# Stationary weights of the first MLP projection: every other column, a distance of its own for each unit

## The chip, the cores and the metric

The kernel runs on one core of a Trainium2 chip. The metric is the device time of one execution in microseconds; it is the median of several runs. TensorE (PE) multiplies: a weight load (PEld) puts a block of 128 x 128 into the array, the *stationary* operand, and a matmul then streams up to 512 columns of the *moving* operand past it, with sums in PSUM. VectorE (DVE) and ScalarE (ACT) prepare operands and take results out, GpSimd (POOL) does little here, and SyncE (SP) issues the transfers from HBM to SBUF.

## The reference

One decoder layer for 256 positions of width 2048, in fp32. A combined projection feeds three branches (gated DeltaNet, HGRN2, attention into 256 memory tokens), which are gated, added and projected; then follows the MLP, which the change is about:

```python
        h2 = rmsnorm(x, g_pre_mlp[l])
        m = jnp.square(jax.nn.relu(h2 @ w_mlp_in[l])) @ w_mlp_out[l]
        x = x + rmsnorm(m, g_post_mlp[l])
```

`w_mlp_in` is 2048 x 8192, `w_mlp_out` 8192 x 2048.

## The kernel before

**Two halves of each number.** Each fp32 operand is split into a high part (rounded to the fast matmul format, `fp32r`) and a low part, the rest. A product is high x high + high x low + low x high. ACT makes the high part (a cast), DVE the low part (a subtraction); for weights these are `wh`, `wl`, or in the MLP `oh`, `ol`, for the normed activations `h2h` holds both parts side by side.

**The first projection.** It has 16 *units* of 512 columns of `w_mlp_in`; two units make an *e* of 1024 columns, and there are eight of these. In unit 0 the activations are stationary. In units 1 to 15 (`unit_stacked`) the weights are stationary. The 16 blocks of 128 rows (index `kt`) come two to a *group* (`KG = 2`), so a unit has 8 groups, loaded by a DMA of 512 KB each into one of six `raw` buffers. `products_joined` works on two groups at a time. For each of the four column blocks `c` and each `kt` there is a *wide* product, the high block against 512 columns (the high and the low activations), and a *narrow* one, the low block against the 256 columns of the high activations. Wide ones of both groups come in a row of 32, then narrow ones in a row of 32, and the next pair of groups in turned order, so that wide follows wide. A unit has 64 wide and 64 narrow products; 15 units have 960 of each. Block `c` of a group is `wh[:, j, c * P:(c + 1) * P]`, 128 adjacent columns.

**Where operands lie.** In the built program every moving buffer, `h2h`, starts at a place in the partition that leaves the remainder 128 modulo 256 bytes, and so does each high tile. The low tile has some columns to spare, and `shifted` lets it start `o` elements later: 16 elements (64 bytes) in this projection (`aside`), 0 in the second one. `pair_at` makes the six pairs of tiles that all MLP weights go through in turn, `operand` hands out the next.

**What becomes of the result.** PSUM bank `c` holds block `c` of the unit, with hidden columns as partitions and positions as columns. ACT and DVE add its halves, apply the squared ReLU, and split it into `mh` and `ml`. These are the stationary operands of the second projection, whose moving operands are rows of `w_mlp_out`: partition i of block `c` must meet the row that belongs to the same hidden column. `raw` loads two blocks of 128 rows side by side, `(k p) n -> p k n`: partition p holds row p of each block. Part of the second projection goes through seven products of sums of quadrants instead of eight (`seven`), which also go through `raw`. Unit 0 has its result with positions as partitions, and `gen_turn` transposes it on PE.

**Order.** The engines each run their own stream of instructions, recorded in program order with background work (`bg`, `tick`) let in between groups; transfers of the MLP weights are all on SP's queue. The second projection of one e stands behind the first projection of the next.

Of the kernel before, what the change touches and what calls it, by code (L numbers as in the profile page):

```python
# [11 lines left out]
F32R = mybir.dt.float32r  # L12
# [5 lines left out]
P = 128  # L18
D = 2048
S = 256  # L20
# [13 lines left out]
KG = 2  # L34
# [6 lines left out]
def tile_trunk(ctx: ExitStack, tc, a):  # L41
    nc = tc.nc
# [21 lines left out]
    V, A, T = Placed(nc.vector), Placed(nc.scalar), Placed(nc.tensor)  # L64
# [25 lines left out]
    def nm(s):  # L90
        cnt[0] += 1
        return f"{s}_{cnt[0]}"

    def g4(name, shape=(P, 1024), dt=F32):
        return gp.tile(list(shape), dt, tag="g", name=nm(name))
# [14 lines left out]
    def const(name, shape, dt=F32):  # L110
        return cst.tile(list(shape), dt, tag=name, name=name)
# [6 lines left out]
    ident = const("ident", [P, P])  # L118
# [69 lines left out]
    def tick(share=1.0):  # L188
        credit[0] += rate[0] * share
        n = int(credit[0])  # L190
        credit[0] -= n
        pump(n)
# [12 lines left out]
    def shifted(t, o):  # L205
        return t[:, o:o + KG * 512].rearrange("p (k n) -> p k n", k=KG)
# [3 lines left out]
    def low(aside):  # L210
        t = wp.tile([P, KG * 512 + 32], F32R, tag="wl", name=nm("wl"))
        odd = low_turn[0] % 2
        low_turn[0] += 1
        return shifted(t, 16 if aside else 32 * odd)

    def split_w(w, n, width=512, step=None, q=lambda i: i, home=None, aside=False):
        if home:
            wh, wl = home(aside)
        else:
            wh = wp.tile([P, KG, 512], F32R, tag="wh", name=nm("wh"))  # L220
            wl = low(aside)
        for j in range(0, n, step or n):
            js = slice(j, min(j + (step or n), n))
            q(A.copy(wh[:, js, 0:width], w[:, js, 0:width]))
            q(V.tensor_tensor(out=wl[:, js, 0:width], in0=w[:, js, 0:width],
                              in1=wh.bitcast(F32)[:, js, 0:width], op=ALU.subtract))
        return wh, wl

    def load_w(src, k0, n, c0, width=512, home=None, aside=False):
        return split_w(load_w_raw(src, k0, n, c0, width), n, width, home=home, aside=aside)  # L230

    def unit(act, nk, src, c0, r0=0, order=None, split=False, post=None, ws=None, load=None):

        if split:
            ps = [bank("mm") for _ in range(2)]
        else:
            both = pmm.tile([P, 1024], F32, tag="mm", name=nm("mm"))  # L240
            ps = [both[:, 0:512], both[:, 512:1024]]
        if order is None:
            order = [(g, None) for g in range(nk // KG)]
        ws = ws or {}
        for i, (g, tt) in enumerate(order):
            k0 = g * KG
            if g not in ws:
                ws[g] = load(src, r0 + k0, c0) if load else load_w(src, r0 + k0, KG, c0)
            wh, wl = ws[g]
            for j in range(KG):  # L250
                kt = k0 + j
                ah, al = act(kt)
                for t in range(NT) if tt is None else (tt,):
                    o = ps[t]
                    st, sl = ah[:, t * P:(t + 1) * P], al[:, t * P:(t + 1) * P]
                    T.matmul(o, st, wh[:, j, :], start=kt == 0, stop=False)
                    T.matmul(o, st, wl[:, j, :], start=False, stop=False)
                    T.matmul(o, sl, wh[:, j, :], start=False, stop=kt == nk - 1)
            tick()
            if post is not None and i + 1 in post:  # L260
                post[i + 1](ps)
        return ps if split else both

    def products_joined(ps, groups, nk, cs, turned):

        for wide in (0, 1) if turned else (1, 0):
            for k0, (wh, wl), both in groups:  # L270
                for c in cs:
                    for j in range(KG):
                        end = k0 + j == nk - 1 and wide == turned
                        if wide:
                            T.matmul(ps[c], wh[:, j, c * P:(c + 1) * P], both[j], start=k0 + j == 0, stop=end)
                        else:
                            T.matmul(ps[c][:, 0:S], wl[:, j, c * P:(c + 1) * P], both[j][:, 0:S], start=False, stop=end)
                yield

    def flat(b):  # L280
        return b.rearrange("p s n -> p (s n)")

    def unit_stacked(pairs, nk, src, c0, ps, load, ws):

        for gg in range(0, nk // KG, 2):
            groups = []
            for g in (gg, gg + 1):
                k0 = g * KG
                groups.append((k0, ws[g] if g in ws else load(src, k0, c0, True),
                               [flat(pairs[kt // 4][:, kt % 4]) for kt in range(k0, k0 + KG)]))  # L290
            for i, _ in enumerate(products_joined(ps, groups, nk, range(4), gg // 2 % 2)):
                tick(0.5)


# [35 lines left out]
    def split_psum(ps, hi, lo):  # L330
        A.copy(hi, ps)
        V.tensor_tensor(out=lo, in0=ps, in1=hi.bitcast(F32), op=ALU.subtract)
# [297 lines left out]
    for u in range(2):  # L630
        ps = unit(mem_act, KT, w_kv, 1024 + 512 * u) if u else first_unit(w_kv, 1024)
# [7 lines left out]
    for u in range(2):  # L639
        k = unit_joined(lambda kt: memB[kt // 2][:, kt % 2], w_kv, 512 * u)  # L640
# [664 lines left out]
    for hg in range(2):  # L1305
        k, g = forget(unit_joined(hboth, w_in, OFF_BF + 512 * hg), hg)
        q = unit_joined(hboth, w_in, OFF_BQ + 512 * hg)
        own_table(A.activation(q, q, AF.Silu))
        ps = unit(hact, KT, w_in, OFF_BI + 512 * hg)
# [73 lines left out]
    ahead = {}  # L1383

    def first_weights(ps):
        for g in range(2):
            ahead[g] = load_w(a["w_mlp_in"][0], g * KG, KG, 0,
                              home=lambda aside: tuple(g4(n, (P, KG, 512), F32R) for n in ("wh", "wl")))

    for c in range(4):  # L1390
        ys.append(g4("y1", (P, NT, 512)))
        if c < 3:
            ps = unit(mact, KT, a["w_out"][0], 512 * c)
# [6 lines left out]
        else:  # L1400
# [3 lines left out]
            ps = unit(mact, KT, a["w_out"][0], 512 * c, order=last, split=True,  # L1404
                      post={8: first_weights, 11: lambda ps: mix_last(ps, 0)})
# [23 lines left out]
    def at(pool, tag, dt):  # L1429
        return pool.tile([P, KG, 512], dt, tag=tag, name=tag, bufs=1)  # L1430

    def pair_at(pool, i):
        return at(pool, f"oh{i}", F32R), pool.tile([P, KG * 512 + 64], F32R, tag=f"ol{i}", name=f"ol{i}", bufs=1)

    pairs = [pair_at(wx, i) for i in range(2)]
    raws = [at(wx, "raw0", F32)]

    def wide_ring():
        for g in range(2):
            w = load_w_raw(a["w_mlp_in"][0], g * KG, KG, 512)  # L1440
            ahead[8 + g] = split_w(w, KG, home=operand, aside=True)
        weights.close()
        wy = ctx.enter_context(tc.tile_pool(name="wy", bufs=1, side="right", reuse_waits="tile"))
        raws.extend(at(wy, f"raw{i}", F32) for i in range(1, 5))
        raws.append(g4("raw5", (P, KG, 512)))
        pairs.extend(pair_at(wy, i) for i in range(2, 6))

    def operand(aside):
        pairs.append(pairs.pop(0))
        return pairs[-1][0], shifted(pairs[-1][1], 16 if aside else 0)  # L1450

    def raw(src, k0, c0):
        w = raws.pop(0)
        raws.append(w)
        nc.sync.dma_start(w, src[k0 * P:(k0 + KG) * P, c0:c0 + 512].rearrange("(k p) n -> p k n", p=P))
        return w

    def load_in(src, k0, c0, aside=False):
        return split_w(raw(src, k0, c0), KG, home=operand, aside=aside)

    h2act = act_of(h2T)
    stf = const("stf", [P, 8])
    out_r = a["out"][0].rearrange("(t p) n -> p t n", p=P)
    NE = DFF // 1024
    first = [(g, t) for t in range(NT) for g in range(4)] + [(g, None) for g in range(4, 8)]
    w_mo = a["w_mlp_out"][0]

    def gen_turn(r, rT, hi, lo):

        yield  # L1470
        pt = pmm.tile([P, 1024], F32, tag="mm", name=nm("mT"))
        for hh in range(2):
            for q in range(2):
                for t in range(NT):
                    k = t * 4 + hh * 2 + q
                    T.transpose(pt[:, hh * 512 + q * S + t * P:hh * 512 + q * S + (t + 1) * P],
                                r[:, k * P:(k + 1) * P], ident)
            p3 = pt[:, hh * 512:(hh + 1) * 512].rearrange("p (q s) -> p q s", q=2)
            split_psum(p3, hi[:, hh * 2:hh * 2 + 2, :], lo[:, hh * 2:hh * 2 + 2, :])
            A.copy(rT[:, hh * 2:hh * 2 + 2, :], p3)  # L1480
            yield
# [221 lines left out]
```

## Time and profile before

| | us |
|---|---|
| median of 3 runs (1776.69 to 1779.16) | 1776.71 |
| profiled execution, device time | 1777.77 |
| its span, first to last instruction | 1776.0 |
| PE busy | 1761.3 |
| weight loads busy (they overlap PE) | 1495.8 |
| DVE busy | 1303.4 |
| ACT busy | 961.8 |
| first projection, units 1 to 15: from start 1098.7 to 1682.8, between output products | 960 wide, 960 narrow |

A group's row in the profile names what was written, then what was read, the moving operand ahead of the stationary one: `mm<-h2h,oh` is a wide product, `mm<-h2h,ol` a narrow one. Behind the shape (rows * columns of the array, then the output) stand the count, the time in which at least one of the group was running, the mean length of one in ns, and the idle time ahead of them with what ended it. Lengths of matmuls overlap, since the next starts while one drains; the pitch from start to start is what counts, and it is read from the timeline.

### The profile page before, as it was taken

What the parts mean: (1) busy time and instruction counts of PE and PEld (TensorE: products, weight loads), DVE (VectorE), ACT (ScalarE), POOL (GpSimd) and SP (SyncE); (2) the same over time, 40 slices, a digit from 0 to 9 for tenths busy, and PEclk for the clock granted to TensorE, in tenths of its full rate; (3) what the DMA queues carried; (4) which work ended last, traced back from release to release, by engine and by line L of the source; (5) the groups of instructions that cost most, each with busy time, mean ns of one, the idle gap of its engine ahead of it and who ended that gap; (6) DMA issues with size and microseconds to landing.
All of it is one profiled execution on the core that took longest, in us unless ns stands there. A gap on an engine that the chain in (4) does not pass through costs nothing.

```text
span 1776.0 us, 23962 instructions
## 1 busy us (share of the span) xinstructions
PE 1761.3 (99%) x9053; PEld 1495.8 (84%) x9053; DVE 1303.4 (73%) x1764; ACT 961.8 (54%) x1217; POOL 58.0 (3%) x100
## 2 busy tenths in 40 slices
PE   9999999999999999999999999999999999999998
PEld 7888888888888888888888888888888888888886
DVE  6765768685859487698555557796979797969796
ACT  6644666454555475565444445665545464646453
POOL 1000000400030000000000000000000000000000
PEclk9999999999999999999999999999999999999999
DMA  8665555875587465555666665767767676767683
GB/s 265 214 193 166 168 160 165 220 216 159 161 216 210 135 190 166 158 174 168 188 189 189 235 222 198 233 228 237 229 226 249 220 250 214 257 204 250 212 295 144
DMA packets 188804, 362.84 MB, mean 204 GB/s; under 512 B 14456, under 2 KB 16272, under 8 KB 188304
## 3 DMA queue, kind: packets, MB, share of 16 engines
q1 hardware_dynamic: 181856, 351.32, 62.2%
q0 software_dynamic: 2304, 5.44, 1.5%
q10 hardware_dynamic: 4528, 4.54, 0.9%
q8 instruction: 71, 1.16, 0.3%
q14 instruction: 45, 0.37, 0.1%
HBM read 356.86 MB, written 4.39 MB: 203 GB/s over the span
## 4 chain that ended last, share of the span: by engine, by line
PE 77%; DVE 5%; issue 2%; DMA 1%; ACT 1%; DVEq 0%; POOLq 0%; POOL 0%; ACTq 0%
PE mm L56 73%; DVE ol L56 3%; PE pa L56 1%; DMA raw<-in_w_mlp_out 1%; DVE relu L56 1%; DVE raw L56 1%; PE kk L56 0%; DVE ml L56 0%; PE bo L56 0%; PE o L56 0%; PE pzt L56 0%; PE pw L56 0%; PE tr L56 0%; PE y L56 0%; PE oT L56 0%
## 5 line engine op out<-in xcount | busy, mean ns | idle before, releaser
L56 DVE TENSOR_TENSOR wl<-w,wh 128x1024 fp32r<-128x1024 f32 (+1 forms) x362 | 436.7, 1217 | 234.9 <-ACT wh L56 212.7
L56 ACT CAST wh<-w 128x1024 fp32r<-128x1024 f32 (+1 forms) x362 | 375.5, 1047 | 354.6 <-PE mm L56 293.2
L56 ACT CAST oh<-raw 128x1024 fp32r<-128x1024 f32 x288 | 299.3, 1053 | 274.8 <-PE mm L56 195.8
L56 DVE TENSOR_TENSOR ol<-raw,oh 128x1024 fp32r<-128x1024 f32 x288 | 343.2, 1221 | 95.5 <-ACT oh L56 65.3
L56 PE MATMUL mm<-wh,hh 128*128 128x512 f32 x1152 | 366.2, 392 | 0.0
L56 PEld LDWEIGHTS mm<-wh,hh 128*128 128x128 f32 x1152 | 216.1, 188 | 44.6 <-ACT wh L56 0.3
L56 PE MATMUL mm<-wl,hh 128*128 128x512 f32 x576 | 224.5, 390 | 0.0
L56 PE MATMUL mm<-h2h,oh 128*128 128x512 f32 x960 | 224.3, 390 | 0.0
L56 PEld LDWEIGHTS mm<-h2h,oh 128*128 128x128 f32 x960 | 178.1, 188 | 35.8
L56 PE MATMUL mm<-hh,wh 128*128 128x512 f32 x768 | 184.6, 391 | 0.8 <-ACT z L56 0.8
L56 PEld LDWEIGHTS mm<-hh,wh 128*128 128x128 f32 x768 | 140.6, 188 | 28.3 <-ACT z L56 1.0
L56 PE MATMUL mm<-ol,mh 128*128 128x512 f32 x372 | 145.3, 391 | 1.6 <-DVE ol L56 1.6
L56 PE MATMUL mm<-oh,mh 128*128 128x512 f32 x372 | 145.4, 391 | 0.0
L56 PE MATMUL mm<-oh,ml 128*128 128x512 f32 x372 | 143.8, 389 | 0.0
L56 PEld LDWEIGHTS mm<-wl,hh 128*128 128x128 f32 x576 | 108.2, 188 | 21.2
L56 PEld LDWEIGHTS mm<-h2h,ol 128*128 128x128 f32 x960 | 117.4, 189 | 3.0 <-DVE ol L56 0.7
L56 PE MATMUL mm<-h2h,ol 128*128 128x256 f32 x960 | 118.5, 281 | 0.5 <-DVE ol L56 0.5
L56 PEld LDWEIGHTS mm<-hh,wl 128*128 128x128 f32 x768 | 97.1, 188 | 3.4
L56 PE MATMUL mm<-hh,wl 128*128 128x256 f32 x768 | 99.7, 280 | 0.0
L56 PEld LDWEIGHTS mm<-ol,mh 128*128 128x128 f32 x372 | 69.8, 188 | 17.8 <-DVE ol L56 3.7
L56 PEld LDWEIGHTS mm<-oh,mh 128*128 128x128 f32 x372 | 69.8, 188 | 16.1 <-DVE acc L56 1.6
L56 PEld LDWEIGHTS mm<-oh,ml 128*128 128x128 f32 x372 | 69.8, 188 | 14.4
(363 smaller groups left out, 2208.7 us busy)
## 6 DMA issues: line engine op xcount, KB each, us to landing
w<-in_w_in SPq DMA_DIRECT2D x240, 512.0 KB, 4.2
raw<-in_w_mlp_out SPq DMA_DIRECT2D x170, 512.0 KB, 4.6
raw<-in_w_mlp_in SPq DMA_DIRECT2D x118, 512.0 KB, 4.8
w<-in_w_out SPq DMA_DIRECT2D x32, 512.0 KB, 4.2
w<-in_w_kv_mem SPq DMA_DIRECT2D x30, 512.0 KB, 5.0
w<-in_w_br_c SPq DMA_DIRECT2D x16, 512.0 KB, 3.6
w<-in_w_br_a SPq DMA_DIRECT2D x16, 512.0 KB, 4.3
w<-in_w_br_b SPq DMA_DIRECT2D x16, 512.0 KB, 3.6
```

What stands on the lines that cost most here:

```text
L56: ins = op(*args, **kwargs)
```

## The change

The stationary block `c` of a unit's group takes every other column of a half of 256: column 256 (c // 2) + 2 i + (c mod 2) for i = 0 to 127, a step of 8 bytes in SBUF. Both tiles of a pair now have 64 spare elements, and `places` gives each unit two starts, in elements, for its high and its low tile: units 1 to 7 have the same one for both, 8 to 56, which is 32 to 224 bytes from the moving operand modulo 256; units 8 to 15 have 0 to 56 for the high tile and 32 more, modulo 64, for the low one. Odd blocks start one element further. Since a partition of the result now stands for another hidden column, the rows of `w_mlp_out` are loaded `(p k) n -> p k n`: partition p holds rows 2p and 2p + 1 of the 256. The transpositions of unit 0's result read every other column too. The arithmetic is the same.

On every engine the changed program has the same instructions on the same buffers in the same order with the same waits.

```diff
@@ -213,9 +213,9 @@
         low_turn[0] += 1
         return shifted(t, 16 if aside else 32 * odd)
 
-    def split_w(w, n, width=512, step=None, q=lambda i: i, home=None, aside=False):
+    def split_w(w, n, width=512, step=None, q=lambda i: i, home=None, aside=False, place=None):
         if home:
-            wh, wl = home(aside)
+            wh, wl = home(place or (0, 16 if aside else 0))
         else:
             wh = wp.tile([P, KG, 512], F32R, tag="wh", name=nm("wh"))
             wl = low(aside)
@@ -261,7 +261,13 @@
                 post[i + 1](ps)
         return ps if split else both
 
-    def products_joined(ps, groups, nk, cs, turned):
+    def plain(w, c):
+        return w[:, c * P:(c + 1) * P]
+
+    def every_other(w, c):
+        return w.rearrange("p (q i r) -> p q r i", q=2, r=2)[:, c // 2, c % 2, :]
+
+    def products_joined(ps, groups, nk, cs, turned, part=plain):
 
 
 
@@ -272,13 +278,16 @@
                     for j in range(KG):
                         end = k0 + j == nk - 1 and wide == turned
                         if wide:
-                            T.matmul(ps[c], wh[:, j, c * P:(c + 1) * P], both[j], start=k0 + j == 0, stop=end)
+                            T.matmul(ps[c], part(wh[:, j, :], c), both[j], start=k0 + j == 0, stop=end)
                         else:
-                            T.matmul(ps[c][:, 0:S], wl[:, j, c * P:(c + 1) * P], both[j][:, 0:S], start=False, stop=end)
+                            T.matmul(ps[c][:, 0:S], part(wl[:, j, :], c), both[j][:, 0:S], start=False, stop=end)
                 yield
 
     def flat(b):
         return b.rearrange("p s n -> p (s n)")
+
+    places = [(0, 0), (8, 8), (16, 16), (24, 24), (32, 32), (40, 40), (48, 48), (56, 56),
+              (0, 32), (8, 40), (16, 48), (24, 56), (32, 0), (40, 8), (48, 16), (56, 24)]
 
     def unit_stacked(pairs, nk, src, c0, ps, load, ws):
 
@@ -286,9 +295,9 @@
             groups = []
             for g in (gg, gg + 1):
                 k0 = g * KG
-                groups.append((k0, ws[g] if g in ws else load(src, k0, c0, True),
+                groups.append((k0, ws[g] if g in ws else load(src, k0, c0, places[c0 // 512]),
                                [flat(pairs[kt // 4][:, kt % 4]) for kt in range(k0, k0 + KG)]))
-            for i, _ in enumerate(products_joined(ps, groups, nk, range(4), gg // 2 % 2)):
+            for i, _ in enumerate(products_joined(ps, groups, nk, range(4), gg // 2 % 2, every_other)):
                 tick(0.5)
 
 
@@ -1385,7 +1394,7 @@
     def first_weights(ps):
         for g in range(2):
             ahead[g] = load_w(a["w_mlp_in"][0], g * KG, KG, 0,
-                              home=lambda aside: tuple(g4(n, (P, KG, 512), F32R) for n in ("wh", "wl")))
+                              home=lambda place: tuple(g4(n, (P, KG, 512), F32R) for n in ("wh", "wl")))
 
     for c in range(4):
         ys.append(g4("y1", (P, NT, 512)))
@@ -1430,7 +1439,7 @@
         return pool.tile([P, KG, 512], dt, tag=tag, name=tag, bufs=1)
 
     def pair_at(pool, i):
-        return at(pool, f"oh{i}", F32R), pool.tile([P, KG * 512 + 64], F32R, tag=f"ol{i}", name=f"ol{i}", bufs=1)
+        return tuple(pool.tile([P, KG * 512 + 64], F32R, tag=f"{t}{i}", name=f"{t}{i}", bufs=1) for t in ("oh", "ol"))
 
     pairs = [pair_at(wx, i) for i in range(2)]
     raws = [at(wx, "raw0", F32)]
@@ -1438,33 +1447,34 @@
     def wide_ring():
         for g in range(2):
             w = load_w_raw(a["w_mlp_in"][0], g * KG, KG, 512)
-            ahead[8 + g] = split_w(w, KG, home=operand, aside=True)
+            ahead[8 + g] = split_w(w, KG, home=operand, place=places[1])
         weights.close()
         wy = ctx.enter_context(tc.tile_pool(name="wy", bufs=1, side="right", reuse_waits="tile"))
         raws.extend(at(wy, f"raw{i}", F32) for i in range(1, 5))
         raws.append(g4("raw5", (P, KG, 512)))
         pairs.extend(pair_at(wy, i) for i in range(2, 6))
 
-    def operand(aside):
+    def operand(place):
         pairs.append(pairs.pop(0))
-        return pairs[-1][0], shifted(pairs[-1][1], 16 if aside else 0)
+        return tuple(shifted(t, o) for t, o in zip(pairs[-1], place))
+
+    w_mo = a["w_mlp_out"][0]
 
     def raw(src, k0, c0):
         w = raws.pop(0)
         raws.append(w)
-        nc.sync.dma_start(w, src[k0 * P:(k0 + KG) * P, c0:c0 + 512].rearrange("(k p) n -> p k n", p=P))
+        order = "(p k) n -> p k n" if src is w_mo else "(k p) n -> p k n"
+        nc.sync.dma_start(w, src[k0 * P:(k0 + KG) * P, c0:c0 + 512].rearrange(order, p=P))
         return w
 
-    def load_in(src, k0, c0, aside=False):
-        return split_w(raw(src, k0, c0), KG, home=operand, aside=aside)
+    def load_in(src, k0, c0, place=None):
+        return split_w(raw(src, k0, c0), KG, home=operand, place=place)
 
     h2act = act_of(h2T)
     stf = const("stf", [P, 8])
     out_r = a["out"][0].rearrange("(t p) n -> p t n", p=P)
     NE = DFF // 1024
     first = [(g, t) for t in range(NT) for g in range(4)] + [(g, None) for g in range(4, 8)]
-    w_mo = a["w_mlp_out"][0]
-
     def gen_turn(r, rT, hi, lo):
 
         yield
@@ -1472,9 +1482,8 @@
         for hh in range(2):
             for q in range(2):
                 for t in range(NT):
-                    k = t * 4 + hh * 2 + q
                     T.transpose(pt[:, hh * 512 + q * S + t * P:hh * 512 + q * S + (t + 1) * P],
-                                r[:, k * P:(k + 1) * P], ident)
+                                every_other(r[:, t * 512:(t + 1) * 512], hh * 2 + q), ident)
             p3 = pt[:, hh * 512:(hh + 1) * 512].rearrange("p (q s) -> p q s", q=2)
             split_psum(p3, hi[:, hh * 2:hh * 2 + 2, :], lo[:, hh * 2:hh * 2 + 2, :])
             A.copy(rT[:, hh * 2:hh * 2 + 2, :], p3)
```

## The prediction

> **What bounds the kernel now.** I read the page first (busy shares), then the table by stages, then the PE timeline of one unit, since the change only touches operands of the first MLP projection.
>
> ```profile
> PE 1761.3 (99%) x9053; PEld 1495.8 (84%) x9053; DVE 1303.4 (73%) x1764; ACT 961.8 (54%) x1217; POOL 58.0 (3%) x100
> PE 77%; DVE 5%; issue 2%; DMA 1%; ACT 1%; DVEq 0%; POOLq 0%; POOL 0%; ACTq 0%
> ```
>
> PE is busy for 1761.3 of 1776.0 us and carries 77% of the chain of waits. So what the change does to the pitch at which PE starts its matmuls goes to the end of the kernel almost one to one. One unit of the projection, and the stretch of output products after its second unit, by the table of stretches (columns: span, PE busy, PEld busy, DVE, ACT, POOL, granted clock, DMA share, GB/s):
>
> ```profile
> 1212.88:1234.97 22.09, 22.09 (x130) 19.55 (x128) 11.33 (x13) 9.49 (x12) 0.00 (x0) 1.00 0.69 225
> 1163.00:1209.00 46.00, 44.88 (x199) 36.71 (x199) 38.70 (x39) 31.20 (x39) 0.00 (x0) 1.00 0.77 261
> ```
>
> In a unit PE has no gap at all, at full clock (1.00), while DVE and ACT are busy for 11.33 and 9.49 of 22.09 us: they keep up even if PE gets 10% faster, and DMA at a share of 0.69 does too. So only the pitch counts. It is read from the timeline, where equal matmuls merge (start, length, count):
>
> ```profile
> 1115.33 3.93 PE L56 MATMUL mm<-h2h,ol 128*128 128x256 f32 x32
> 1119.10 7.44 PE L56 MATMUL mm<-h2h,oh 128*128 128x512 f32 x32
> 1126.38 3.93 PE L56 MATMUL mm<-h2h,ol 128*128 128x256 f32 x32
> ```
>
> From start to start: 32 narrow products (256 columns of h2h moving, a low weight block stationary) take 1119.10 - 1115.33 = 3.77 us, **117.8 ns** each; 32 wide ones (512 columns, high block) 7.28 us, **227.5 ns** each. The groups of the whole run:
>
> ```profile
> L56 PE MATMUL mm<-h2h,oh 128*128 128x512 f32 x960 | 224.3, 390 | 0.0
> L56 PE MATMUL mm<-h2h,ol 128*128 128x256 f32 x960 | 118.5, 281 | 0.5 <-DVE ol L56 0.5
> L56 PEld LDWEIGHTS mm<-h2h,ol 128*128 128x128 f32 x960 | 117.4, 189 | 3.0 <-DVE ol L56 0.7
> L56 PEld LDWEIGHTS ab<-hh,wabs 128*32 128x32 f32 x32 | 3.4, 108 | 0.3
> ```
>
> 960 of each, 960 x (227.5 + 117.8) = 331 us, 18.7% of the span. One ns on both pitches is 1.9 us. How far are these pitches from what the streams need? 256 more moving columns make a matmul 390 - 281 = 109 ns longer, 0.426 ns a column: 512 columns need 218 ns, 256 need 109. A weight load is 189 ns for 128 columns and 108 ns for 32: 81 / 96 = 0.84 ns a column, 107 ns for 128, each with its start. Loads alone, without a moving stream to speak of, show in four products of 8 columns:
>
> ```profile
> 168.08 0.37 PE L56 MATMUL te<-ld,caus 128*128 128x8 f32 x2
> 168.30 0.36 PE L56 MATMUL mm<-hh,wl 128*128 128x256 f32 x1
> ```
>
> Two of them take 0.22 us: 110 to 112 ns a load. So a wide product runs 9.5 ns above its stream, and a narrow one 5.8 ns above the load. Both excesses come while two streams read SBUF together, and that is what the change aims at.
>
> **The change part by part.** No instruction is added, removed or moved: on each of the five engines the rows, their buffers and their waits are the same, so there is no queue to be moved past and no new wait. Four properties of operands change.
>
> 1. *Stride of the stationary block.* A load takes 0.84 ns a column. With adjacent columns it advances 4 bytes per 0.84 ns while the moving stream advances 4 bytes per 0.426 ns; the two run at unequal speed through SBUF and pass each other during the load. With every other column the load advances 8 bytes per 0.84 ns, the speed of the moving stream: both walk in step and their distance stays what the unit's place makes it. If the excess is a collision of the two streams at equal places modulo 256 bytes, which no row proves, it either goes away or recurs, by place.
>
> 2. *Distance.* Before, every high block starts at the remainder modulo 256 bytes of the moving buffer, every low one 64 bytes further (`aside`). After, units 1 to 7 have both at 32, 64 ... 224 bytes, units 8 to 15 the high ones at 0 to 224 and the low ones 128 from that. So the result is a mean over 15 places. What the place and the phase of the streams do at the present stride is to be seen in other stretches:
>
> ```profile
> 109.90 1.64 PE L56 MATMUL mm<-hh,wl 128*128 128x256 f32 x13
> 170.25 0.28 PE L56 MATMUL sc<-ckh,cqh 128*128 128x256 f32 x1
> 170.61 0.28 PE L56 MATMUL sc<-ckh,cqh 128*128 128x256 f32 x1
> 1119.10 1.32 PE L56 MATMUL mm<-h2h,oh 128*128 128x512 f32 x5
> 153.75 3.87 PE L56 MATMUL ab<-hh,wabs 128*32 128x256 f32 x32
> ```
>
> The first run has low blocks at 64 or 192 bytes: (1.64 - 0.28) / 12 = 113.3 ns. The sc products have both operands at the same remainder: three starts in 0.36 us, 120 ns. The first five wide products of a group: (1.32 - 0.39) / 4 = 232.5 ns, before they settle at 227. So the same shapes run at 113 to 120 ns, and 227 to 232 ns, by how the streams meet; something of the excess is theirs to lose. Against it stands the last row: with loads of only 32 columns the narrow pitch is still (3.87 - 0.28) / 31 = 116 ns, so most of its excess may belong to the moving stream alone.
>
> The bounds: all excess gone, (9.5 + 5.8) x 960 = 14.7 us less. All places as bad as the worst rows, (232.5 - 227.5 + 120 - 117.8) x 960 = 6.9 us more. Between them I take half of the gain, **7.3 us**: as though half of the 15 places were free of collisions and the rest as now. The row nearest to it is the one at 113.3 ns, which shows that an undisturbed narrow product exists; nothing shows a wide one at 218.
>
> *Could a load with stride 2 be slower?* No row has one. The nearest is the load for a transposition:
>
> ```profile
> L56 PEld LDWEIGHTS tr<-ident,x 128*128 128x128 f32 x64 | 7.2, 141 | 1.2 <-DVE x L56 0.6 <-DVE h2h L56 0.2
> ```
>
> 128 adjacent columns in 141 ns instead of 188 to 189: taking off the same start (108 - 32 x 0.84 = 81 ns), 60 ns for 512 bytes, 8.5 bytes a ns. With stride 2 a load spans 1024 bytes in 107 ns, 9.6 bytes a ns, about as much. So I take no loss here. If it takes twice as long, 214 ns and some 5 of start, the narrow pitch becomes 219: (219 - 117.8) x 960 = 97 us more, with the wide one just still covered; it begins to cost beyond 0.88 ns a column, where 128 columns and 5 ns reach 117.8.
>
> [...]
>
> 3. *ACT and DVE write to shifted places.* All low tiles of the projection are already written 64 bytes off, those of the output products are not, and they are in one row:
>
> ```profile
> L56 DVE TENSOR_TENSOR ol<-raw,oh x288: 1214/1220/1228, 1104.0 to 1752.4; 128x1024 fp32r<-128x1024 f32 x144
> ```
>
> Minimum, median and maximum are within 14 ns, so a shift costs DVE nothing; for ACT's casts I take the same. The cover, PE's 22.09 us against 11.33, is wide in any case. The eight strided transpositions of unit 0 are 8 loads; at twice 60 ns they would cost 0.5 us.
>
> 4. *Rows of the second matrix.* Each partition now takes rows 2p and 2p + 1 of a block of 256 instead of p and p + 128; size and number of pieces stay.
>
> ```profile
> raw<-in_w_mlp_out SPq DMA_DIRECT2D x170, 512.0 KB, 4.6
> raw<-in_w_mlp_in SPq DMA_DIRECT2D x118, 512.0 KB, 4.8
> w<-in_w_out SPq DMA_DIRECT2D x32, 512.0 KB, 4.2
> 1506.53 3.97 DMA raw<-in_w_mlp_out
> 1592.30 3.94 DMA raw<-in_w_mlp_out
> ```
>
> Matrices with rows of 32 KB and of 8 KB land in 4.8 and 4.2 us, so the order of rows should move the landing by less than 0.6 us. Six buffers and PE's work cover it; in the stretch 1163 to 1209 PE lacks only 1.1 us. Where the chain of waits goes through this load (the two last rows), 0.6 us each would be 1.2 us. I take 0.
>
> Sum: the profiled execution took 1777.77 us around its span of 1776.0; the median of the runs is 1776.71. 1777.77 - 7.3 = 1770.5 on its scale, **1769.4 us** on that of the median.
>
> **The rivals.**
>
> *B, nothing changes* (1776.7). The excess belongs to the moving stream, whatever the load reads: for it the 32-column row (116 ns with a quarter of the load), against it 113 and 120 ns for one shape. At most the 1.8 ns between 117.8 and 116 would be won, 1.7 us.
>
> [...]
>
> *C, walking in step makes it worse* (slower). Two streams that meet once now stay together through the whole load; places where they meet run at the worst pitches seen, 232.5 and 120 ns. All 15 places: 6.9 us more, 1783.6; ten of them, 4.6 us, 1781.3. It decides from the point where the bad places outweigh the good ones: a place without any excess wins 14.7 / 15 = 0.98 us, a worst one loses 0.46. The five slow products at each start of a wide group, which settle to 227 only as the streams drift apart, speak for it: in step nothing drifts.
>
> *D, the strided load is slower* (1873.7 if twice as long; 1790 at 0.99 ns a column). Against it stands the row of the transposition's load.
>
> **How the numbers follow.** A, part of the excess goes: 0.42. B: 0.21. C: 0.23. D: 0.14. A measurement tells 0.2%, 3.6 us, from no change, so faster is A, slower is C and D: 0.42, 0.21, 0.37. A's own range is from 1762.0 (no excess left) to 1773.1. The range takes in B and C and a little of D, from 1761 to 1787; D proper is left out.
>
> **What would show it.** In the timeline of the changed kernel each unit has its own pair of pitches. A: some units at 218 to 222 and 112 to 114 ns, others as now. B: all at 227 and 118. C: units above 230 and 120. D: the weight-load group of h2h,ol well above 189 ns and narrow pitches above 120 in every unit alike. Landing of raw from in_w_mlp_out above 5.2 us, or more idle time of PE from 1163 to 1209, would show step 4 wrong. What would make the forecast wrong is that the excess is not a meeting of the two streams at all, or that nearly all places are bad.

## The result: slower by half a per cent

The changed kernel takes 1786.78 us (median of 4 runs, 1786.27 to 1787.83), the kernel before in the same series 1777.93 us (4 runs, 1776.69 to 1779.47). The ratio is 1.0050, with a 95% interval of 1.0033 to 1.0068: slower, beyond the 0.2% that a measurement can tell. The forecast was 1769.4 us, and its sign is wrong.

### The profile after

The page of the changed kernel: span, busy shares, the weight loads and products of the projection, and the landing of the two weight matrices.

```profile
span 1785.3 us, 23962 instructions
PE 1769.2 (99%) x9053; PEld 1505.7 (84%) x9053; DVE 1302.7 (73%) x1764; ACT 961.3 (54%) x1217; POOL 58.6 (3%) x100
...
L56 PE MATMUL mm<-h2h,oh 128*128 128x512 f32 x960 | 229.1, 394 | 0.0
L56 PEld LDWEIGHTS mm<-h2h,oh 128*128 128x128 f32 x960 | 185.2, 195 | 33.4
...
L56 PEld LDWEIGHTS mm<-h2h,ol 128*128 128x128 f32 x960 | 120.1, 196 | 2.8 <-DVE ol L56 0.6
L56 PE MATMUL mm<-h2h,ol 128*128 128x256 f32 x960 | 121.0, 284 | 0.4 <-DVE ol L56 0.4
...
raw<-in_w_mlp_out SPq DMA_DIRECT2D x170, 512.0 KB, 5.1
raw<-in_w_mlp_in SPq DMA_DIRECT2D x118, 512.0 KB, 4.8
```

The engines run as many instructions as before, and PE is busy 7.9 us longer. The weight loads of the projection went from 188 to 189 ns to 195 or 196, and the second matrix lands in 5.1 us instead of 4.6. The timeline of PE, one piece of unit 2 and one of unit 7 (start, length, count):

```profile
1127.88 4.00 PE L56 MATMUL mm<-h2h,ol 128*128 128x256 f32 x32
1131.72 7.53 PE L56 MATMUL mm<-h2h,oh 128*128 128x512 f32 x32
1139.09 4.01 PE L56 MATMUL mm<-h2h,ol 128*128 128x256 f32 x32
...
1323.90 4.00 PE L56 MATMUL mm<-h2h,ol 128*128 128x256 f32 x32
1327.74 7.63 PE L56 MATMUL mm<-h2h,oh 128*128 128x512 f32 x32
1335.21 4.00 PE L56 MATMUL mm<-h2h,ol 128*128 128x256 f32 x32
```

From start to start, unit 2 has 3.84 us for 32 narrow products, 120.0 ns each, and 7.37 us for 32 wide ones, 230.3 ns. Unit 7 has 120.0 and 233.4 ns. Before, every unit had 227.4 and 117.8. Read so for all units (means over all of a unit's products of a shape; places are the distance of the high and of the low block from the moving buffer, modulo 256 bytes; unit 1 starts with a wait and its narrow mean is left out):

```
unit        1     2     3     4     5     6     7     8     9     10    11    12    13    14    15
high/low  32/32 64/64 96/96  128   160   192   224  0/128 32/160 64/192 96/224 128/0 160/32 192/64 224/96
wide ns   231.9 230.2 230.2 231.4 233.3 233.4 233.6 233.3 232.1 230.3 233.5 231.7 233.4 233.0 233.8
narrow ns   -   120.1 120.7 120.4 120.2 120.7 120.0 120.9 120.1 120.7 120.5 119.7 120.0 119.8 120.9
```

No place has a wide pitch at or below 227.4, and none a narrow one at or below 117.8. The means are 232.3 and 120.3 ns. By the number of products, the wide ones cost 960 x 4.9 ns = 4.7 us and the narrow ones 960 x 2.5 = 2.4 us. The table of stretches says the same as a sum over the 15 units (span, then the engines' busy time), first of before, then of the changed kernel:

```profile
sum 329.94, PE 329.42 PEld 291.37 DVE 234.11 ACT 158.39 POOL 0.00; mean PE 21.96 PEld 19.42 DVE 15.61 ACT 10.56 POOL 0.00
```

```profile
sum 337.02, PE 336.59 PEld 301.16 DVE 233.97 ACT 158.53 POOL 0.00; mean PE 22.44 PEld 20.08 DVE 15.60 ACT 10.57 POOL 0.00
```

So 7.1 of the 9.3 us by which the span grew lie in the units, and there PE has no idle time to speak of in either kernel. The rest: 1.0 us lies ahead of unit 1, in code that did not change (that start lay between 1097.6 and 1099.7 us in most of the profiles below); 1.2 us lie behind unit 15 (93.3 before, 94.5 now); the six long stretches of output products between units took 252.29 us before and 252.19 now.

### The profile page after: what moved, and what is told of

Its sections match the earlier page's. It is cut to its first block, busy times and chain, and to the rows that moved or that the text cites. A ratio compares the mean times of both kernels' runs of the same rounds, so it can differ in the third digit from the quotient of the medians.

```text
span 1785.3 us, 23962 instructions
## 1 busy us (share of the span) xinstructions
PE 1769.2 (99%) x9053; PEld 1505.7 (84%) x9053; DVE 1302.7 (73%) x1764; ACT 961.3 (54%) x1217; POOL 58.6 (3%) x100
## 4 chain that ended last, share of the span: by engine, by line
PE 70%; DVE 6%; issue 4%; DMA 4%; ACT 1%; POOL 1%; DVEq 0%; POOLq 0%; ACTq 0%
PE mm L56 66%; DVE ol L56 3%; DMA raw<-in_w_mlp_out 2%; PE pa L56 1%; DVE relu L56 1%; DVE raw L56 1%; DMA w<-in_w_in 1%; DVE ml L56 1%; DMA lb<-scr 0%; DMA scr<-U 0%; DMA raw<-in_w_mlp_in 0%; PE o L56 0%; PE bo L56 0%; DVE wl L56 0%; PE pzt L56 0%
## 5 line engine op out<-in xcount | busy, mean ns | idle before, releaser
L56 PE MATMUL mm<-h2h,oh 128*128 128x512 f32 x960 | 229.1, 394 | 0.0
L56 PEld LDWEIGHTS mm<-h2h,oh 128*128 128x128 f32 x960 | 185.2, 195 | 33.4
L56 PEld LDWEIGHTS mm<-h2h,ol 128*128 128x128 f32 x960 | 120.1, 196 | 2.8 <-DVE ol L56 0.6
```

What stands on the lines that cost most here:

```text
L56: ins = op(*args, **kwargs)
```

## Experiments

Three theories stood at the start. **S**: it is the stride of the block's columns that costs. **P**: it is the places; 0 for the high and 64 for the low block, as before, were a good pair, and the sweep leaves it. **R**: the new order of rows costs something of its own. Kernels that were run several times have an interval. The others were run once, and of these mainly the units are read, since the executions of the kernel before themselves lie between 1775.9 and 1781.5 us in these series. Of each diff only the lines that matter most are shown; where the columns are called adjacent or the rows as before, the lines that bring that back are left out.

### One part of the change alone

*dist_only*: the sweep of places as in the change, columns adjacent, rows as before. Against the changed kernel:

```diff
-            for i, _ in enumerate(products_joined(ps, groups, nk, range(4), gg // 2 % 2, every_other)):
+            for i, _ in enumerate(products_joined(ps, groups, nk, range(4), gg // 2 % 2)):
-        order = "(p k) n -> p k n" if src is w_mo else "(k p) n -> p k n"
+        order = "(k p) n -> p k n"
-                                every_other(r[:, t * 512:(t + 1) * 512], hh * 2 + q), ident)
+                                plain(r[:, t * 512:(t + 1) * 512], hh * 2 + q), ident)
```

> Only the starts of the tiles change, by unit, as in the change; blocks of adjacent columns, rows of the second matrix as before. Theory S (the stride costs, since a strided block touches twice the bytes of SBUF in a load, 1024 instead of 512): every unit at 227.4 and 117.8 ns within 1 ns, load 188 ns, time 1776.7 within 2 us. Theory P (the place costs, whatever the stride): units spread as in the changed kernel, wide 230 to 234, narrow near 120, time near 1784.

Measured: 1780.94 us against 1778.35, ratio 1.0015 (1.0005 to 1.0025). Its units:

```
unit        1     2     3     4     5     6     7     8     9     10    11    12    13    14    15
high/low  32/32 64/64 96/96  128   160   192   224  0/128 32/160 64/192 96/224 128/0 160/32 192/64 224/96
wide ns   233.0 233.2 234.1 232.6 233.2 229.0 233.2 227.8 233.1 233.2 234.0 232.5 233.4 229.1 233.1
narrow ns   -   115.7 117.5 118.5 120.1 115.6 117.3 120.1 119.9 117.8 117.7 119.6 118.3 113.5 117.3
```

The timeline of unit 14, 192 and 64 bytes:

```profile
1643.37 3.79 PE L56 MATMUL mm<-h2h,ol 128*128 128x256 f32 x32
1647.00 7.49 PE L56 MATMUL mm<-h2h,oh 128*128 128x512 f32 x32
1654.33 3.79 PE L56 MATMUL mm<-h2h,ol 128*128 128x256 f32 x32
```

3.63 us for 32 narrow products are 113.4 ns, 7.33 us for 32 wide ones 229.1. So place does count with adjacent columns. For the wide product, only 0 (227.8) and 192 (229) are good, all others cost 232.5 to 234; the mean is 232.3, the very mean of the changed kernel. For the narrow one the mean is 117.8, that of the kernel before. So P holds for the wide product; for the narrow one, which it expected near 120, it doesn't, as 64 bytes was an average place there. The time, too, lies between what the two theories expected.

*stride_only*: every other column, rows to match, but the places of before in all units.

```diff
-    places = [(0, 0), (8, 8), (16, 16), (24, 24), (32, 32), (40, 40), (48, 48), (56, 56),
-              (0, 32), (8, 40), (16, 48), (24, 56), (32, 0), (40, 8), (48, 16), (56, 24)]
+    places = [(0, 16)] * 16
```

> Every other column in all units, but at the distances of the kernel before (high 0, low 64 bytes). Theory S: wide 230 to 234 and narrow 119 to 121 in every unit, load 195 ns, time near 1785. Theory P: 227.4 and 117.8, load 188, time near 1777, since no place has changed.

Measured: 1786.58 us, ratio 1.0045 (1.003 to 1.006), about the whole of the loss. Timeline of unit 2 and the group of loads:

```profile
1126.95 4.00 PE L56 MATMUL mm<-h2h,ol 128*128 128x256 f32 x32
1130.79 7.64 PE L56 MATMUL mm<-h2h,oh 128*128 128x512 f32 x32
1138.26 4.00 PE L56 MATMUL mm<-h2h,ol 128*128 128x256 f32 x32
...
L56 PEld LDWEIGHTS mm<-h2h,oh 128*128 128x128 f32 x960 | 183.4, 194 | 36.0
```

120.0 ns and 233.4 ns, in all units alike. So with every other column the good place is gone: at 0 the wide product takes 233.6 where adjacent columns take 227.4. The two edits don't add on the wide product, since each alone already brings it to 232 to 234; they share one loss. On the narrow product, by the means, only the stride costs.

*rows_only*: the kernel before, with the rows of the second matrix in the new order; the columns aren't changed to match.

```diff
-        nc.sync.dma_start(w, src[k0 * P:(k0 + KG) * P, c0:c0 + 512].rearrange("(k p) n -> p k n", p=P))
+        order = "(p k) n -> p k n" if src is w_mo else "(k p) n -> p k n"
+        nc.sync.dma_start(w, src[k0 * P:(k0 + KG) * P, c0:c0 + 512].rearrange(order, p=P))
```

> The kernel before, but the rows of the second matrix loaded two adjacent ones to a partition (so they meet the wrong hidden columns: this kernel leaves the matching of rows out). Theory S and P: pitches as before, landing of these loads 5.1 instead of 4.6 us, hidden by the buffers, time 1777 within 1.5 us. Theory R (the rest of the loss that the pitches leave, some 2 us, is the later landing): 1779.

Measured: 1780.41 us, ratio 1.0012 (1.0003 to 1.0021). Landing, and then the waits from 1163 us to 1776 (total us, times, longest):

```profile
raw<-in_w_mlp_out SPq DMA_DIRECT2D x170, 512.0 KB, 5.2
...
ACT oh L56 <- DMA raw<-in_w_mlp_out: 46.6, 35, 3.6
```

The same row of the kernel before:

```profile
ACT oh L56 <- DMA raw<-in_w_mlp_out: 28.3, 27, 2.7
```

The rows cost about 2 us by themselves: landing is 0.6 us later, and ACT, which casts what has landed, waits 18 us longer for it in all, most of it under PE's work. Sums over the six output stretches, of rows_only, then of dist_only, then of before, then of the changed kernel:

```profile
sum 254.82, PE 250.49 PEld 202.13 DVE 241.67 ACT 160.07 POOL 0.00; mean PE 41.75 PEld 33.69 DVE 40.28 ACT 26.68 POOL 0.00
```

```profile
sum 249.74, PE 249.09 PEld 202.51 DVE 240.42 ACT 161.21 POOL 0.00; mean PE 41.51 PEld 33.75 DVE 40.07 ACT 26.87 POOL 0.00
```

```profile
sum 252.29, PE 249.57 PEld 202.41 DVE 242.12 ACT 160.81 POOL 0.00; mean PE 41.60 PEld 33.73 DVE 40.35 ACT 26.80 POOL 0.00
```

```profile
sum 252.19, PE 249.90 PEld 202.57 DVE 241.51 ACT 160.87 POOL 0.00; mean PE 41.65 PEld 33.76 DVE 40.25 ACT 26.81 POOL 0.00
```

Span less PE is PE's idle time in these stretches: 4.3 us in rows_only, 0.7 in dist_only, 2.7 before, 2.3 after. The four form a square: new rows add 2.5 us where the units are as before (252.3 to 254.8) and 2.5 where the units are longer (249.7 to 252.2); longer units take off 2.6 with either order. A reading that fits is that a longer unit gives the loads behind it more time, and an output stretch then waits less; then the rows did cost in the changed kernel, and the longer units gave as much back. It is PE that lost less; ACT still waited for these loads in the changed kernel:

```profile
ACT oh L56 <- DMA raw<-in_w_mlp_out: 43.6, 37, 3.7
```

The exchange is likely, but its size is not shown. Each corner of the square is one profile, and that of dist_only is its fastest execution, 2.1 us under its own median, so its 249.7 may be low. Two kernels below with the old rows, dist_two and stride_narrow, have units 1.4 and 2.0 us longer than before, and their output stretches are not shorter but 0.6 us longer. The median of dist_only agrees in kind: it rose by 2.6 us where the units grew by 4.6.

### Where stride begins to cost

*stride_four*: as stride_only, with every fourth column of 512 (16 bytes a step) and the rows to match.

```diff
-        return w.rearrange("p (q i r) -> p q r i", q=2, r=2)[:, c // 2, c % 2, :]
+        return w.rearrange("p (i r) -> p r i", r=4)[:, c, :]
```

> Every fourth column of 512 (16 bytes a step, each column in another 16-byte piece), high at 0, low at 64 bytes, rows of the second matrix to match. Theory S (bytes or pieces touched): the excess grows again, wide 236 to 242, narrow 123 to 135, load above 200 ns, some 10 to 20 us over the kernel before. Theory L (only walking in step at the speed of the moving stream costs): at 16 bytes a column the streams pass each other again, so 227 to 229 and 118, load 188, time near 1778.

Measured: 1889.21 us. The loads of the low block and the timeline of unit 5:

```profile
L56 PEld LDWEIGHTS mm<-h2h,ol 128*128 128x128 f32 x960 | 226.5, 328 | 0.0
...
1233.52 7.51 PE L56 MATMUL mm<-h2h,ol 128*128 128x256 f32 x32
1240.87 7.80 PE L56 MATMUL mm<-h2h,oh 128*128 128x512 f32 x32
1248.51 7.52 PE L56 MATMUL mm<-h2h,ol 128*128 128x256 f32 x32
```

By rows of 32 a narrow product takes 229.7 ns and a wide one 238.8 here, as in the other units. With the start of 81 ns that the prediction took off, the load needs an estimated (328 - 81) / 128 = 1.9 ns a column, 247 ns in all, far more than the 109 ns that the prediction estimated for the moving stream of a narrow product; so by estimate the narrow product waits for its load. The estimate is a little high: 247 ns of loading are more than the pitch of 229.7. The expectations were too low. This is what rival D described, at a step of 16 bytes instead of 8, and its price for a doubled load, 97 us, is near the 111 measured. The span grew by 111.5 us where the units grew by 117.3; the output stretches, at 247.4, gave 4.9 back.

By the groups of loads of before, of the changed kernel and of this one, a high block takes 188 ns at four bytes a step, 195 at eight and 311 at sixteen, a low one 189, 196 and 328: the first doubling of the step costs 7 ns a load, the second 116 to 132.

*stride_narrow*: every other column for the low blocks alone, places of before. The matching of the columns of high and low blocks is left out. The edit also reaches the low blocks of an earlier projection, which go through `products_joined` too.

```diff
-                            T.matmul(ps[c][:, 0:S], part(wl[:, j, :], c), both[j][:, 0:S], start=False, stop=end)
+                            T.matmul(ps[c][:, 0:S], every_other(wl[:, j, :], c), both[j][:, 0:S], start=False, stop=end)
```

> Every other column for the narrow products alone, at distances 0 and 64 bytes; adjacent columns for the wide ones, rows as before (so columns of high and low part do not match: their matching is left out). Theory S: the two costs are apart: wide 227.4 with a load of 188 ns, narrow 120 with one of 194 to 196, 2 us over the kernel before. Rival: the narrow ones' phase spoils the wide ones too, 230 or more.

Measured: 1783.78 us, of which 3.4 lie ahead of unit 1. The groups of loads in the units:

```profile
L56 PEld LDWEIGHTS mm<-h2h,oh 128*128 128x128 f32 x960 | 178.0, 188 | 35.8
...
L56 PEld LDWEIGHTS mm<-h2h,ol 128*128 128x128 f32 x960 | 119.7, 194 | 2.9 <-DVE ol L56 0.6
```

Pitches: wide 227.6, narrow 119.7. So each product pays for its own block's stride, whatever its neighbours read. The earlier projection shows the same once more. Its 768 narrow products, before and then here:

```profile
L56 PE MATMUL mm<-hh,wl 128*128 128x256 f32 x768 | 99.7, 280 | 0.0
L56 PEld LDWEIGHTS mm<-hh,wl 128*128 128x128 f32 x768 | 97.1, 188 | 3.4
```

```profile
L56 PE MATMUL mm<-hh,wl 128*128 128x256 f32 x768 | 102.2, 284 | 0.0
L56 PEld LDWEIGHTS mm<-hh,wl 128*128 128x128 f32 x768 | 99.8, 196 | 3.3
```

The load rose from 188 to 196 ns and the products' busy time by 2.5 us, most of the 3.4 us ahead of unit 1.

### What the place is, and whether a better one pays

*dist_two*: adjacent columns; high blocks at 0 in units 1 to 8 and at 192 in units 9 to 15, the low ones swept behind each.

```diff
+    places = [(0, 0), (0, 0), (0, 8), (0, 16), (0, 24), (0, 32), (0, 40), (0, 48), (0, 56),
+              (48, 0), (48, 8), (48, 16), (48, 24), (48, 32), (48, 40), (48, 56)]
```

> Adjacent columns, rows as before; the high tile at 0 in units 1 to 8 with the low one at 0 to 224 bytes (unit 2 at 32, unit 8 at 224), at 192 bytes in units 9 to 15 with the low one at 0 to 160 and 224. Theory M (the narrow pitch hangs on the low tile's place and on the phase that the wide products ahead leave): wide 227.4 in the first eight and 229 in the others whatever the low tile, narrow from 113 to 120, lower behind 192. Theory W (each product's pitch hangs on its own place alone): narrow equal at equal low places in both halves.

Measured: 1779.6 us; by place of the low block:

```
low block                 0     32    64    96    128   160   192   224
narrow ns, high at 0     120   118.3 117.8 117.4 120.1 119.9 117.7 116.6
narrow ns, high at 192   119.3 118.1 113.5 117.4 120.1 119.8   -   116.7
wide ns, high at 0       227.6 228.4 227.4 227.0 227.6 227.6 228.1 227.8
wide ns, high at 192     229.0 228.8 229.0 228.9 229.1 232.3   -   230.3
```

Mostly a product's pitch goes by its own block's place. Two things stand out: 64 bytes is 113.5 behind a high block at 192, 117.8 behind one at 0 and, in dist_only, 115.7 behind one at 64; and the last two units of the second row of wide products are 1 to 3 ns slow. Both blocks' places count together there; why isn't known.

*moving_shift*: the moving buffers start 64 bytes later. The tiles in odd units are moved along (0 and 64 remain), those in even units stay where they are (so 192 and 0).

```diff
+    const("pad", [P, 16])
+    places = [(0, 16), (16, 32)] * 8
+        back = 48 if any(pairs[-1][0] is t for t in left) else 0
+        return tuple(shifted(t, (o + back) % 64) for t, o in zip(pairs[-1], place))
```

> Adjacent columns; the moving buffers start 64 bytes later (remainder 192 modulo 256). In odd units the tiles move along, so the distances stay 0 and 64; in even units the tiles stay where the kernel before has them, so the distances are 192 and 0. Theory D (the distance to the moving operand counts): odd units 227.4 and 117.8, even ones 229 and 119.3 as at that pair in the sweep. Theory A (the tiles' own place counts): even units 227.4 and 117.8, odd ones 233.2 and 119, as at 64 and 128 bytes.

Measured: 1805.97 us, of which 20.7 lie ahead of unit 1, where the pad moves the operands of all earlier stages too (the 1152 products `mm<-wh,hh` take 372.9 us there, 366.2 before). Units 4 and 5:

```profile
1233.80 3.98 PE L56 MATMUL mm<-h2h,ol 128*128 128x256 f32 x32
1237.62 7.49 PE L56 MATMUL mm<-h2h,oh 128*128 128x512 f32 x32
1244.94 3.98 PE L56 MATMUL mm<-h2h,ol 128*128 128x256 f32 x32
...
1256.05 3.93 PE L56 MATMUL mm<-h2h,ol 128*128 128x256 f32 x32
1259.82 7.44 PE L56 MATMUL mm<-h2h,oh 128*128 128x512 f32 x32
1267.10 3.93 PE L56 MATMUL mm<-h2h,ol 128*128 128x256 f32 x32
```

Odd units keep 227.4 and 117.8 at their new addresses; even ones have 229 to 230 and 119.3 to 119.6, dist_two's figures for 192 and 0, though their tiles didn't move. So it is the distance to the moving operand that counts here, not the address.

*place_high192*: the best pair seen, 192 and 64, in all units, adjacent columns, rows of before.

```diff
+    places = [(48, 16)] * 16
```

> Adjacent columns, rows as before, all units with the high tile at 192 and the low one at 64 bytes, the best unit of the sweep. Theory M: every unit 229.1 and 113.5 ns, 15 x 64 x 2.6 ns = 2.5 us off the units; the stretches of output products give up to 1.4 us of it back, as they got shorter by 2.6 us where the units were 4.6 us longer: 1 to 2.5 us under the kernel before. Rival: 113.5 came from what the unit before left; then 117.8 and a time 1.6 us over it.

Measured: 1777.11 us (11 runs) against 1778.14 (15), ratio 0.9993 (0.9984 to 1.0002). Every unit has 229.0 and 113.5 ns, and the units together are 2.4 us shorter. The output stretches are 1.5 us longer than before (253.8 against 252.3). That may be the same exchange as above in the other direction, and no gain can be told: the interval reaches from 2.8 us less to 0.4 us more.

*more_raw*: the kernel before with a seventh buffer for landed weights, to see whether earlier loads lift the output stretches. The room came from the pads of the low tiles, which then lie 64 bytes off in the second projection too.

```diff
-        raws.extend(at(wy, f"raw{i}", F32) for i in range(1, 5))
+        raws.extend(at(wy, f"raw{i}", F32) for i in (1, 2, 3, 4, 6))
```

> The kernel before with a seventh buffer for raw weights; to make room the low tiles have no spare columns and lie 64 bytes off in the second projection too. Pitches of the first projection 227.4 and 117.8. If the gaps of the output products are late landings, the six stretches fall from 252.3 to about 247.5 us in sum, the kernel by 4 to 5 us, to 1773.5. If they are DVE's or ACT's own lateness, nothing changes.

Measured: 1794.79 us, ratio 1.0089 (1.0073 to 1.0106). It settles nothing on the loads: the pitch of the output products rose from 227 to 232 ns at their new places, and the order of buffers brought one stall of PE in unit 2, in the waits from 1098 to 1176 us:

```profile
PE mm L56 <- ACT oh L56: 9.9, 1, 9.9
```

### Does the excess come from the load beside it?

*short_loads*: places and columns of before, but only the first 64, 96 or 32 columns of each block (by unit, in turn) except in the first and last product of a sum; the other columns of the products are left out.

```diff
+                        m = P if end or (wide and k0 + j == 0) else n
-                            T.matmul(ps[c], wh[:, j, c * P:(c + 1) * P], both[j], start=k0 + j == 0, stop=end)
+                            T.matmul(ps[c][0:m], wh[:, j, c * P:c * P + m], both[j], start=k0 + j == 0, stop=end)
```

> The kernel before, but weight blocks of 64, 96 and 32 columns in units 1, 2, 3 and so on in turn (the rest of each product is left out, except first and last ones of a bank). Theory S (the excess comes from the load and the matmul reading SBUF together): wide near 220 with 32 columns, 222 with 64, 225 with 96, narrow 110 to 114. Theory B (it belongs to the moving stream): wide 226 to 228 in all, narrow 116 with 32 columns.

*short_strided*: the same with every other column.

> Every other column at the distances 0 and 64 bytes, but blocks of 64, 96 and 32 columns in units 1, 2, 3 and so on in turn (the rest of each product is left out, except first and last ones of a bank). Adjacent columns gave 117.4, 116.7 and 118.8 ns narrow, 230.8, 231.5 and 230.2 wide. Theory F (a narrow product with stride 2 waits for its longer load, 195 instead of 188 ns): with a load of 96 columns or fewer, which is over in time, the narrow pitch falls to that of adjacent columns, within 0.5 ns. Theory G (the strided load disturbs the moving stream, whatever its length): narrow 119 to 121 also with 96 and 64 columns, wide above 232.

Measured: 1779.33 us for short_loads and 1781.33 for short_strided. Timeline of short_loads, the end of unit 4 (64 columns) and the start of unit 5 (96):

```profile
1216.78 7.53 PE L56 MATMUL mm<-h2h,oh 128*64 128x512 f32 x32
1224.14 3.97 PE L56 MATMUL mm<-h2h,ol 128*64 128x256 f32 x32
1227.95 7.55 PE L56 MATMUL mm<-h2h,oh 128*64 128x512 f32 x32
1235.33 3.92 PE L56 MATMUL mm<-h2h,ol 128*96 128x256 f32 x32
1239.09 7.53 PE L56 MATMUL mm<-h2h,oh 128*96 128x512 f32 x32
```

```
columns of a block            128    96     64     32
adjacent: load ns             188    161    135    108
          wide, narrow ns     227.4  230.8  230.3  231.5
                              117.8  117.4  118.8  116.7
every other: load ns          195    166    136    108
          wide, narrow ns     233.6  230.8  230.8  233.3
                              120.0  118.5  115.8  114.9
```

With adjacent columns a load of a quarter of the columns leaves the excess where it was: 116.7 against 117.8 narrow, and wide even 4 ns more, which neither theory expected. So the excess over the stream is not the time in which the load reads beside it. With every other column the narrow product does follow the load's length, 120.0 down to 114.9, and it is slower than the adjacent one just where the strided load is longer, by 5 to 7 ns at 96 and 128 columns. A floor by the load would explain 128 columns: by estimate 195 - 81 = 114 ns of loading and the 5 of start are 119, and no unit of the changed kernel is below 119.7, while adjacent loads allow 112 and reached 113.5. It doesn't explain 96 columns, where by the same estimate the load needs 166 - 81 + 5 = 90 ns, and the same estimate gives 252 ns for stride_four, where 229.7 were measured. So the floor is argued, not shown; what is shown is that with 128 columns the stride makes the narrow product 2 ns slower.

## Why the prediction was wrong

**The bound was right.** In the units PE has hardly a gap in either kernel (0.5 us of 329.9 before, 0.4 of 337.0 after), ACT and DVE kept up, and the pitches carry the loss: 7.1 of 9.3 us. The cover was thinner than in the one unit that the prediction read, where DVE was busy for 11.3 us. In every odd unit from 3 on DVE is busy for 18 to 20 of 21.9 us before, as in unit 13:

```profile
1575.16:1597.03 21.87, 21.87 (x129) 19.37 (x127) 18.88 (x20) 10.58 (x14) 0.00 (x0) 1.00 0.59 190
```

Had the pitches become 10% shorter, 19.7 us a unit, DVE would hardly have kept up there.

**"Almost one to one" is doubtful.** dist_only's units grew by 4.6 us and its median by 2.6, with an interval of 0.9 to 4.4; place_high192 saved 2.4 and had no gain that can be told. The output stretches, which had 2.7 us of PE idle, may take up part of what the units win or lose. The prediction read those stretches at one row and left them out of the sum.

**The step that failed is the term of 7.3 us saved.** The excess of 9.5 and 5.8 ns was taken for a meeting of the two streams which half of the places would be rid of, and the places before for no better than others. The prediction named this as a premise that no row proves, and had a row against it, the loads of 32 columns with 116 ns. short_loads shows that this row was the one to follow: the excess doesn't shrink with the load. In place of 7.3 us less, the pitches measured 4.9 + 2.5 ns more, 7.1 us.

**The bounds held, the choice between them didn't.** The upper bound, all places as bad as the worst rows, was 232.5 and 120 ns or 6.9 us; the units averaged 232.3 and 120.3. So rival C's price for 15 bad places, 6.9 us, was nearly the 7.1 measured in the units. That is in part luck: its 120 ns came from products with both operands at the same place, while the narrow products here got there with the stride. Its mechanism, streams in step that stay together, no run shows. The wide product loses the same 4.9 ns by the sweep alone, where by the prediction's estimates (0.84 ns a column for the load, 0.426 for the moving stream) nothing walks in step: it loses because 0 was the best of the eight places tried. That the place before might be a good one already was missing. The prediction costed the other places by rows of other products, as though the units' own were an average.

**The stride.** Zero was taken, with 0.88 ns a column as the point where it begins to cost. The load rose by 7 ns, (195 - 81) / 128 = 0.89 ns a column: just past that point, and the narrow product shows it with 119.7 to 120.9 ns in every unit but the first, 2.4 us. Rival D was right in kind and far off in price for this step; something near its doubling came with every fourth column. The row of the transposition's load was a better guide than the prediction made of it. Its 8.5 bytes a ns give an estimate of 1024 / 8.5 = 120 ns for this step and 241 for sixteen bytes; with the same start of 81 ns taken off, 114 and 230 to 247 were measured. The prediction read 9.6 against 8.5 as about as much, and by this estimate the narrow product's loss lay in that difference.

**Rival B.** That the excess belongs to the moving stream, whatever the load reads, fits short_loads, where less loading freed nothing (narrow 116.7 ns with 32 columns loaded, 117.8 with 128). But for B place would do nothing, and that isn't so: with adjacent columns 227.4 ns at a distance of 0 and 232.5 or more at all others but 192, with a distance that follows the moving buffer in moving_shift (227.4 in odd units, 229 to 230 in even ones).

**The shifted writes** cost nothing that shows: DVE's sum over the units is 234.0 us after and 234.1 before, ACT's 158.5 and 158.4.

**The rows** were taken at 0 and cost some 2 us where nothing covers them (1.0012, 1.0003 to 1.0021). The bound of 0.6 us a landing held (0.5 to 0.6), but not the count of places where it shows: two rows of the chain were taken, while ACT waited for this load 27 times before and 35 with the new rows. In the changed kernel the longer units seem to have kept it from PE.

**Still open**: where the 9 ns above the stream of a wide product come from, why 0 and 192 are better than other distances, why a strided block has no such good place, how far the output stretches answer a longer unit, and the 1.2 us behind the last unit, which stride_only shows too (94.3) and rows_only doesn't (93.4).

## What to carry to other kernels

A small excess over an ideal rate is not yet something that can be won: before paying for a rearrangement, shorten the suspected partner (here the load) and see whether the excess moves. A setting that every unit shares may be the best of its kind, so the mean over a sweep of settings may well be worse than it; one look at the sweep by itself prices that. And when a stage's time changes, ask what the stage behind it does with the time, since its waits for loads may give back or take away part of it.

## What the runs showed of the hardware

- In this projection the pitch of equal products goes by the distance, modulo 256 bytes and tried in steps of 32, between stationary and moving operand: with adjacent columns about 227.4 ns at 0, mostly 229 at 192 (two units of dist_two had 230.3 and 232.3), 232.5 to 234 at six others (512 columns moving), and 113.5 to 120.1 with 256. With adjacent columns a shorter load hardly lowers it: 231.5 and 116.7 ns with 32 columns loaded, where 128 have 227.4 and 117.8.
- A load of 128 columns of this projection's weights, 4 bytes each, takes 188 or 189 ns with adjacent columns, 194 to 196 with every other, and 311 to 328 with every fourth.
- The landing of 512 KB of `w_mlp_out` in pieces of 2 KB goes, by the median, from 4.6 to 5.1 or 5.2 us when a partition takes two neighbouring rows instead of two that lie 128 apart.
